# A hybrid decoder block on one core: the first norm by quarters behind the splitting of x, and one metered queue per stage for the work between weight units

## The chip, the core and the metric

The program runs on one core of a Trainium2 chip. A core has TensorE (PE, the matrix engine; its weight loads are shown apart as PEld), VectorE (DVE), ScalarE (ACT), GpSimd (POOL) and SyncE (SP, which here only issues DMAs). Each has its own instruction queue and works through it in order; they wait for each other by semaphores. The metric is the device time of one execution in microseconds (us). Before the change it is 1526.94 us, the median of three runs (1526.02 to 1527.0). What a measurement of this kernel can tell from no change is about 0.2%, or 3 us.

## What is computed

One decoder layer for 256 tokens with 2048 channels, all in float32: an RMSNorm, one large input projection, three parallel branches (an S5 state space, an RG-LRU recurrence and stick-breaking attention) that are gated and merged, an output projection with a residual, a second RMSNorm, an MLP with squared ReLU, and a last RMSNorm.

```python
def rms_norm(x, g):
    y = x * rsqrt(mean(x * x, axis=-1, keepdims=True) + EPS)
    return y * g

xn = rms_norm(x, norm_mix_g)
proj = xn @ w_in                          # 2048 -> 11264 columns
u_s5, u_lru, q, k, v, gate_logits = split(proj)
gates = sigmoid(gate_logits + b_gate)
# RG-LRU: causal conv of width 4, then
r, i = sigmoid(xc @ w_r + b_r), sigmoid(xc @ w_i + b_i)
a = exp(-8 * r * softplus(-lam))
y_lru = linear_scan(a, sqrt(1 - a * a) * (i * xc))
merged = g_s5 * (y_s5 @ w_br_s5) + g_lru * (y_lru @ w_br_lru) + g_attn * (y_attn @ w_br_attn)
h = x + merged @ w_out
hn = rms_norm(h, norm_mlp_g)
hdn = relu(hn @ w_up)                     # 2048 -> 8192
h = h + (hdn * hdn) @ w_down              # 8192 -> 2048
out = rms_norm(h, final_norm_g)
```

## The kernel before

**Units.** All large weights come as one stream of 520 units, each 256 rows by 512 columns of float32 (512 KB, tile `raw`, loaded on SP's queue by L130). Every unit is split in two parts whose sum carries the float32 precision: ACT casts `raw` to `hi` (L146) and DVE writes `lo = raw - hi` (L147). The activations are split in the same way (`xhi`/`xlo`, `hhi`/`hlo` and so on), and PE multiplies hi by hi, lo by hi and hi by lo. `raw`, `hi` and `lo` have three buffers each: `next_unit` (L151) loads up to three units ahead of the one in use and splits up to two ahead. So a unit's cast can start when PE is done with the unit three before it, its `lo` follows the cast, and its next load waits for the `lo` that frees the `raw` buffer.

**Chunks.** A chunk is 512 output columns. `chunk` (L195) puts channels on partitions, with 24 matmuls of 256 columns for a unit; `chunk_tok` (L215) and `pair_tok` (L245) put tokens on partitions, with 12 matmuls of 512 columns. `pair_tok` runs two chunks together, so that their last two units each come at the end. The order is: the two RG-LRU chunks of `w_in` (units 0 to 15), the two S5 chunks (16 to 31), the RG-LRU gate and branch chunks (gate 32 to 39, branch 40 to 43, and so on to 79), q, k and v, the attention gates and branches, the S5 gates and branches (to 231), `w_out` (232 to 263), and four quarters of the MLP, each four `w_up` chunks and four `w_down` chunks (the first `w_up` pair is units 264 to 279).

**Work between the chunks.** Everything else is written as Python generators that are put in the list `side` by `later(gens, rate)` (L164). After each unit's matmuls `pump` (L179) gives every task in that list `rate` steps (a step runs to the next `yield`), placed behind the unit's splits and matmuls. `finish(task)` runs a task to its end at once. So the amount of such work that goes between two `lo` instructions on DVE depends on how many tasks are in the list at that time, their rates, and how much a step holds. The tile scheduler then makes the final order for each engine from this program.

**The places that the change touches.** `norm1` (L349) waits eight units, then `square_sum` (L337) squares all of x in place on ACT and adds it up on DVE; a matmul with ones gives `ps_n1`, `rsqrt_mean` (L327) makes `rstd`, and `lru_in(0)` (L566) scales the first RG-LRU chunk out of PSUM (L373), which frees its two PSUM banks for the third chunk. `lru_half` (L510) is one half of RG-LRU: a convolution (L522, L524), two small matmuls for each 128 channels into `ps_l` (L530, L531), sigmoids (L532, L533), tanh (L537), exp (L542), sqrt (L550), scans (L557). `s5_scan` (L618) begins when the S5 chunks are done: sine tables (L593 to L598), the split of its first inputs into `ux` (L605, L606), and twelve small DMAs `stk<-ux` on SP's queue (L614); its first matmuls, `ps_v` (L638), read `stk`. `s5_load` and `s5_params` fetch S5's parameters and work them out, mostly on POOL.

Matmul results with tokens on partitions are turned into channels on partitions by `blocks` (L712): 16 DVE transposes of 32-row blocks for a chunk (L716), here in steps of four. `split_tok` does it for the merged branches, `residual` for the residual stream (then `residual_split`, L915), and `hidden` (L1005) for relu's output: transposes, the square on ACT (L1008, `hd_hi`), the same product on POOL (L1009), and the difference on DVE (L1012, `hd_lo`). Each chunk makes a `later` task of its own with rate 1.0, so two such tasks run side by side behind a pair.

Of the kernel before, what the change touches and what calls it, by code (L numbers as in the profile page):

```python
# [14 lines left out]
P = 128  # L15
# [31 lines left out]
def hybrid_block(ctx: ExitStack, tc: tile.TileContext, io, out):  # L47
# [142 lines left out]

    def finish(task):
        while step(task):
            pass
# [143 lines left out]
    def square_sum(t):  # L337
        for k in range(0, KT, 4):
            nc.scalar.activation(t[:, k:k + 4, :], t[:, k:k + 4, :], AF.Square)
            if k % 8:  # L340
                yield
        for k in range(0, 8, 4):
            nc.vector.tensor_tensor(t[:, k:k + 4, :], t[:, k:k + 4, :], t[:, k + 8:k + 12, :], ALU.add)
            yield
        for n in (4, 2, 1):
            nc.vector.tensor_tensor(t[:, 0:n, :], t[:, 0:n, :], t[:, n:2 * n, :], ALU.add)
        yield

    def norm1():  # L349
# [38 lines left out]
    def s5_load():  # L388
        nc.sync.dma_start(prm[:, 2, :], repeat(io["s5_log_dt"], 64))
        nc.sync.dma_start(prm[:, 0:2, :], io["s5_lam"])  # L390
        yield
        yield
        yield
        nc.sync.dma_start(cco, io["s5_c"])
        yield
        nc.sync.dma_start(bco, io["s5_b"])
        yield

    def s5_params():
# [3 lines left out]
        for _ in range(3):  # L403
            yield
# [158 lines left out]
    lq = later([lru_params()], 1)  # L563
# [317 lines left out]
    def split_tok(c, mT):  # L881
        yield
# [20 lines left out]
    last = later([split_tok(3, mlp.tile([P, 4, L], F32, tag="reluT", name="mT3", bufs=2))], 1.0)  # L903
# [5 lines left out]
    def ms(kt):  # L909
        if kt >= 12:  # L910
            finish(last)
# [7 lines left out]
    def residual(c):  # L919
        yield  # L920
        yield from blocks(h_tok[:, :, c * CH:(c + 1) * CH], hT[:, 4 * c:4 * c + 4, :], 4)
        for k in range(4 * c, 4 * c + 4):
            residual_split(k)
            if k % 2:
                yield

    rs2 = const.tile([P, 2], F32, name="rs2")
    rq = [None]

    def out_done(c, banks):  # L930
# [3 lines left out]
        rq[0] = later([residual(c)], 1.0)  # L934
# [5 lines left out]
    def hs(kt):  # L940
        if kt >= 12:
            finish(rq[0])
        return hhi[:, kt, :], hlo[:, kt, :]

    def norm2():
        while rq[0][0]:
            yield
        yield from square_sum(hT)
# [56 lines left out]
    def hidden(r, h_, l_, name):  # L1005
        rT = mlp.tile([P, 4, L], F32, tag="reluT", name=f"reluT{name}", bufs=2)
        yield from blocks(r, rT, 4)
        nc.scalar.activation(h_, rT, AF.Square)  # L1008
        nc.gpsimd.tensor_tensor(rT, rT, rT, ALU.mult)  # L1009
        yield  # L1010
        yield
        nc.vector.tensor_tensor(l_, rT, h_.bitcast(F32), ALU.subtract)  # L1012

    for q in range(NQ):
        hd, hq = {}, [None]

        def up_done(cu, banks):
# [9 lines left out]
            hq[0] = later([hidden(r, h_[:, k, :], l_[:, k, :], f"{q}_{c}")], 1.0)  # L1027
# [6 lines left out]
        def hs_(kt):  # L1034
            if kt >= 12:
                finish(hq[0])
# [90 lines left out]
```

## Time and profile before

| what | value |
|---|---|
| median of three runs | 1526.94 us |
| the profiled execution's own time | 1526.19 us |
| its span, first to last instruction | 1524.4 us |
| matmuls, PE | 7518 |
| bytes read from HBM | 282.71 MB, 187 GB/s over the span |
| DVE, ACT, POOL busy | 1172.1, 780.6, 66.3 us |

The profile shows one execution. A busy PE is not a PE at its peak: where the unit's operands are late, the matmuls simply start later, and the count of matmuls in a stretch tells more than the busy time. The program has two regular rhythms, 24 matmuls of 256 columns or 12 of 512 columns for a unit. In a table of stretches, each engine has its busy time with the number of its instructions behind it as (x...); then come the granted clock of TensorE as a share of full speed, the share of the DMA engines' time and the GB/s. In a timeline, a row is: start, duration, engine, line, operation, out<-in, number of merged instructions, and in brackets the idle time before it and what ended it.

### The profile page before, as it was taken

How to read it: one execution, taken by the hardware profiler on the slowest of the kernel's cores; microseconds unless marked ns; L12 is line 12 of the kernel's file. 1: busy time of each engine (PE TensorE's matmuls, PEld its weight loads, DVE VectorE, ACT ScalarE, POOL GpSimd, SP SyncE). 2: the span in 40 equal slices, each digit the busy share in tenths (PEclk: the TensorE clock that was granted, in tenths of full speed). 3: DMA queues.
4: the chain of work that ended last, by engine and by line, in shares of the span. 5: the costliest groups of instructions: out<-in, count | busy, mean ns of one | idle time of the engine just before them, and what ended most of it. 6: DMA issues, size and time to landing. Idle time of an engine off the chain costs nothing.

```text
span 1524.4 us, 19914 instructions
## 1 busy us (share of the span) xinstructions
PE 1492.2 (98%) x7518; PEld 1261.1 (83%) x7518; DVE 1172.1 (77%) x1452; ACT 780.6 (51%) x918; POOL 66.3 (4%) x76
## 2 busy tenths in 40 slices
PE   9898999999999999999999999999999999999997
PEld 9896888989887878987778778888888888888886
DVE  5786988887988989688698886468855787558855
ACT  7568556465765564444345444344433444344443
POOL 5000000000000000000000010000000000000011
PEclk9999999999999999999999999999999999999999
DMA  8554766655665657665756566656666666666564
GB/s 283 169 166 143 230 207 198 190 173 167 176 188 175 209 181 212 190 200 176 269 163 196 159 200 194 193 188 198 195 193 194 193 193 194 193 193 191 184 206 151
DMA packets 88914, 292.41 MB, mean 192 GB/s; under 512 B 12786, under 2 KB 17010, under 8 KB 88562
## 3 DMA queue, kind: packets, MB, share of 16 engines
q1 hardware_dynamic: 88386, 287.93, 61.5%
q10 hardware_dynamic: 432, 3.21, 0.6%
q8 instruction: 59, 0.97, 0.3%
q14 instruction: 37, 0.30, 0.1%
HBM read 282.71 MB, written 2.10 MB: 187 GB/s over the span
## 4 chain that ended last, share of the span: by engine, by line
PE 86%; DVE 7%; ACT 3%; DMA 2%; issue 2%; SPq 0%; DVEq 0%; ACTq 0%
PE mt_w_up L225 6%; PE mt_w_up L226 6%; PE mt_w_up L224 6%; PE mt_w_in L225 6%; PE mt_w_in L226 6%; PE mt_w_in L224 6%; PE mp_w_down L261 4%; PE mp_w_down L260 4%; PE mp_w_down L259 4%; PE mt_w_down L225 4%; PE mt_w_down L224 4%; PE mt_w_down L226 4%; PE mm_w_in L210 4%; PE mm_w_in L208 4%; PE mm_w_in L209 3%; DVE lo L147 3%
## 5 line engine op out<-in xcount | busy, mean ns | idle before, releaser
L147 DVE TENSOR_TENSOR lo<-raw,hi 128x1024 fp32r<-128x1024 f32 (+1 forms) x521 | 651.2, 1253 | 311.8 <-ACT hi L146 308.7
L146 ACT CAST hi<-raw 128x1024 fp32r<-128x1024 f32 (+1 forms) x521 | 545.7, 1049 | 642.5 <-PE mt_w_up L226 116.8
L225 PE MATMUL mt_w_up<-lo,hhi 128*128 128x512 f32 x448 | 174.9, 390 | 4.4 <-DVE lo L147 4.3
L225 PE MATMUL mt_w_in<-lo,xhi 128*128 128x512 f32 x448 | 176.2, 393 | 2.6 <-DVE lo L147 2.4
L224 PE MATMUL mt_w_in<-hi,xhi 128*128 128x512 f32 x448 | 175.9, 396 | 2.9 <-ACT hi L146 2.9
L226 PE MATMUL mt_w_in<-hi,xlo 128*128 128x512 f32 x448 | 175.4, 391 | 0.0
L226 PE MATMUL mt_w_up<-hi,hlo 128*128 128x512 f32 x448 | 174.3, 389 | 0.0
L224 PE MATMUL mt_w_up<-hi,hhi 128*128 128x512 f32 x448 | 174.3, 389 | 0.0
L208 PE MATMUL mm_w_in<-xhi,hi 128*128 128x256 f32 x512 | 146.5, 287 | 4.7 <-DVE rs L331 4.2
L210 PE MATMUL mm_w_in<-xhi,lo 128*128 128x256 f32 x512 | 145.4, 286 | 1.0 <-DVE lo L147 1.0
L209 PE MATMUL mm_w_in<-xlo,hi 128*128 128x256 f32 x512 | 145.5, 285 | 0.0
L716 DVE STREAM_TRANSPOSE reluT<-relu 32x256 f32<-32x256 f32 x256 | 111.5, 436 | 4.2
L208 PEld LDWEIGHTS mm_w_in<-xhi,hi 128*128 128x128 f32 x512 | 99.4, 194 | 5.5 <-issue 4.4
L225 PEld LDWEIGHTS mt_w_in<-lo,xhi 128*128 128x128 f32 x448 | 84.7, 189 | 23.1 <-DVE lo L147 6.5
L225 PEld LDWEIGHTS mt_w_up<-lo,hhi 128*128 128x128 f32 x448 | 84.1, 188 | 23.8 <-DVE lo L147 6.5
L225 PE MATMUL mt_w_down<-lo,hd_hi 128*128 128x512 f32 (+1 forms) x272 | 102.5, 377 | 0.0
L224 PE MATMUL mt_w_down<-hi,hd_hi 128*128 128x512 f32 (+1 forms) x272 | 102.4, 377 | 0.0
L226 PE MATMUL mt_w_down<-hi,hd_lo 128*128 128x512 f32 (+1 forms) x272 | 102.4, 376 | 0.0
L224 PEld LDWEIGHTS mt_w_in<-hi,xhi 128*128 128x128 f32 x448 | 84.4, 189 | 20.8 <-ACT hi L146 3.8
L210 PEld LDWEIGHTS mm_w_in<-xhi,lo 128*128 128x128 f32 x512 | 98.8, 194 | 1.5 <-DVE lo L147 1.4
L260 PE MATMUL mp_w_down<-lo,hd_hi 128*128 128x512 f32 x256 | 99.6, 389 | 0.0
L259 PE MATMUL mp_w_down<-hi,hd_hi 128*128 128x512 f32 x256 | 99.6, 389 | 0.0
(299 smaller groups left out, 2396.8 us busy)
## 6 DMA issues: line engine op xcount, KB each, us to landing
raw<-in_w_in SPq DMA_DIRECT2D x175, 512.0 KB, 4.2
raw<-in_w_up SPq DMA_DIRECT2D x128, 512.0 KB, 3.8
raw<-in_w_down SPq DMA_DIRECT2D x128, 512.0 KB, 3.9
raw<-in_w_out SPq DMA_DIRECT2D x32, 512.0 KB, 4.2
raw<-in_w_br_lru SPq DMA_DIRECT2D x16, 512.0 KB, 4.5
raw<-in_w_br_attn SPq DMA_DIRECT2D x16, 512.0 KB, 4.1
raw<-in_w_br_s SPq DMA_DIRECT2D x16, 512.0 KB, 4.1
stk<-ux SPq DMA_DIRECT2D x96, 64.0 KB, 4.1
```

The costliest lines, as they stand in the source:

```text
L146: anchor["act"] = nc.scalar.copy(h[:, k, :], r[:, k, :]).ins
L147: anchor["dve"] = nc.vector.tensor_tensor(l_[:, k, :], r[:, k, :], h[:, k, :].bitcast(F32), ALU.subtract).ins
L208: nc.tensor.matmul(o, wh[:, kk, s], xh, start=first and ct % 2 == 0, stop=False, skip_group_check=True)
L209: nc.tensor.matmul(o, wh[:, kk, s], xl, start=False, stop=False, skip_group_check=True)
L210: mm = nc.tensor.matmul(o, wl[:, kk, s], xh, start=False, stop=last and ct % 2 == 1, skip_group_check=True)
L224: nc.tensor.matmul(banks[j], xh[:, s], wh[:, a:b], start=kt == 0, stop=False)
L225: nc.tensor.matmul(banks[j], xh[:, s], wl[:, a:b], start=False, stop=False)
L226: return nc.tensor.matmul(banks[j], xl[:, s], wh[:, a:b], start=False, stop=kt == ng * UK - 1)
L259: nc.tensor.matmul(o, xh[:, s], wh[:, kk, :], start=kt == 0, stop=False)
L260: nc.tensor.matmul(o, xh[:, s], wl[:, kk, :], start=False, stop=False)
L261: mm = nc.tensor.matmul(o, xl[:, s], wh[:, kk, :], start=False, stop=kt == ng * UK - 1)
L716: nc.vector.transpose(d_[32 * a:32 * a + 32, :, :, 32 * b:32 * b + 32], s_[32 * b:32 * b + 32, :, :, 32 * a:32 * a + 32])
```

## The change

1. `norm1` no longer waits eight units. It squares x quarter by quarter on ACT, two units apart, and adds each quarter to the first on DVE, so that the small matmul comes three units earlier; `s5_load` starts seven units later and `s5_params` six. The RG-LRU task's rate goes from 1 to 1.15.
2. New helpers: `chained(task, gen)` appends a generator to one queue (and puts the queue in `side` if it isn't there), and sets a flag when that generator is through; `need(task, flag)` steps the queue only until that flag is set. `split_tok`, `residual` and `hidden` go in one queue each, with rates 1.5, 2.0 and 1.8, and their transposes come in steps of two.
3. The second norm's squares and adds go into `residual`, chunk by chunk; `norm2` has only the last two adds.
4. relu's product goes from POOL to DVE, and `ms`, `hs` and `hs_` ask with `need` for the chunk that a k-tile comes from.

```diff
+    def chained(task, gen):
+        flag = [False]
+        def run():
+            yield from gen(flag)
+            flag[0] = True
+        task[0].append(run())
+        if task not in side:
+            task[2] = 0.0
+            side.append(task)
+        return flag
+
+    def need(task, flag):
+        while not flag[0]:
+            assert step(task)
...
     def norm1():
-        for _ in range(8):
-            yield
-        yield from square_sum(xT)
+        yield
+        for k in range(0, KT, 4):
+            sq_ = xT[:, k:k + 4, :]
+            nc.scalar.activation(sq_, sq_, AF.Square)
+            yield
+            if k:
+                nc.vector.tensor_tensor(xT[:, 0:4, :], xT[:, 0:4, :], sq_, ALU.add)
+            yield
+        for n in (2, 1):
+            nc.vector.tensor_tensor(xT[:, 0:n, :], xT[:, 0:n, :], xT[:, n:2 * n, :], ALU.add)
+        yield
...
     def s5_load():
+        for _ in range(7):
+            yield
         nc.sync.dma_start(prm[:, 2, :], repeat(io["s5_log_dt"], 64))
...
         g.memset(ce, 0.0)
-        for _ in range(3):
+        for _ in range(9):
             yield
...
-    lq = later([lru_params()], 1)
+    lq = later([lru_params()], 1.15)
...
     def split_tok(c, mT):
-        yield
-        yield from blocks(m_tok[:, :, c * CH:(c + 1) * CH], mT, 4)
-        split_pair(4 * c, 4, mT)
+        def gen(flag):
+            yield
+            yield from blocks(m_tok[:, :, c * CH:(c + 1) * CH], mT, 2)
+            split_pair(4 * c, 4, mT)
+        return gen
...
+    mq, mf = [deque(), 1.5, 0.0], []
...
-            last = later([split_tok(c, pp.tile([P, 4, L], F32, tag="t3", name=f"mT{c}"))], 1.0)
-    finish(last)
+            mf.append(chained(mq, split_tok(c, pp.tile([P, 4, L], F32, tag="t3", name=f"mT{c}"))))
+    need(mq, mf[2])
...
     def residual(c):
...
+            flag[0] = True
+            sq_ = hT[:, 4 * c:4 * c + 4, :]
+            nc.scalar.activation(sq_, sq_, AF.Square)
+            yield
+            if c:
+                nc.vector.tensor_tensor(hT[:, 0:4, :], hT[:, 0:4, :], sq_, ALU.add)
                 yield
+        return gen
...
-    rq = [None]
+    rq, rfl = [deque(), 2.0, 0.0], {}
...
-        rq[0] = later([residual(c)], 1.0)
+        rfl[c] = chained(rq, residual(c))
...
     def hidden(r, h_, l_, name):
...
+            yield from blocks(r, rT, 2)
+            nc.scalar.activation(h_, rT, AF.Square)
+            nc.vector.tensor_tensor(rT, rT, rT, ALU.mult)
+            yield
+            yield
+            nc.vector.tensor_tensor(l_, rT, h_.bitcast(F32), ALU.subtract)
+        return gen
...
+    hq = [deque(), 1.8, 0.0]
...
-            hq[0] = later([hidden(r, h_[:, k, :], l_[:, k, :], f"{q}_{c}")], 1.0)
+            hf[c] = chained(hq, hidden(r, h_[:, k, :], l_[:, k, :], f"{q}_{c}"))
```

What the change makes of the engines' orders is seen at three places. The first is DVE in `w_out`, behind its pair of chunks; `lo250` is the `lo` of unit 250, L716 are the transposes of the residual, L917 the residual's own split. Before:

```order
L147 TENSOR_TENSOR lo250_6950<-raw250_6921,hi250_6949 128x1024
L716 STREAM_TRANSPOSE hT_6622<-h_tok_6625 32x2x4x32 x4
L147 TENSOR_TENSOR lo251_6972<-raw251_6947,hi251_6971 128x1024
L716 STREAM_TRANSPOSE hT_6622<-h_tok_6625 32x2x4x32 x8
L147 TENSOR_TENSOR lo252_6998<-raw252_6969,hi252_6997 128x1024
L716 STREAM_TRANSPOSE hT_6622<-h_tok_6625 32x2x4x32 x8
L147 TENSOR_TENSOR lo253_7024<-raw253_6995,hi253_7023 128x1024
L917 SCALAR_TENSOR_TENSOR hlo_6624<-hT_6622,par_79,hhi_6623 128x256 x2
L716 STREAM_TRANSPOSE hT_6622<-h_tok_6625 32x2x4x32 x4
L147 TENSOR_TENSOR lo254_7050<-raw254_7021,hi254_7049 128x1024
```

Now (L729 are the transposes, L932 the split):

```order
L147 TENSOR_TENSOR lo250_6952<-raw250_6923,hi250_6951 128x1024
L729 STREAM_TRANSPOSE hT_6622<-h_tok_6625 32x2x4x32 x4
L147 TENSOR_TENSOR lo251_6974<-raw251_6949,hi251_6973 128x1024
L729 STREAM_TRANSPOSE hT_6622<-h_tok_6625 32x2x4x32 x4
L147 TENSOR_TENSOR lo252_6996<-raw252_6971,hi252_6995 128x1024
L729 STREAM_TRANSPOSE hT_6622<-h_tok_6625 32x2x4x32 x2
L147 TENSOR_TENSOR lo253_7020<-raw253_6993,hi253_7019 128x1024
L932 SCALAR_TENSOR_TENSOR hlo_6624<-hT_6622,par_79,hhi_6623 128x256 x4
L147 TENSOR_TENSOR lo254_7043<-raw254_7017,hi254_7042 128x1024
L729 STREAM_TRANSPOSE hT_6622<-h_tok_6625 32x2x4x32 x2
L147 TENSOR_TENSOR lo255_7063<-raw255_7040,hi255_7062 128x1024
```

Before, two chunks' transposes stood together, eight between one `lo` and the next; now there are two or four, and the second chunk's come when the first's are through.

The second place is ACT in RG-LRU's second half; `hi37` is the cast of unit 37, `lru_r1`, `lru_i1`, `lru_tc1` and `lru_ts1` are this half's tiles, `ts0` and `tc0` the first S5 tables. Before, from the cast of unit 37 to that of unit 38, in the first gate chunk:

```order
L146 CAST hi37_1464<-raw37_1435 128x1024
L597 ACT_TABLE_LOAD
L597 ACTIVATE ts0_1403<-ts0_1403 128x1024
L598 ACTIVATE tc0_1402<-tc0_1402,half_pi_131 128x1024
L542 ACT_TABLE_LOAD
L542 ACTIVATE lru_r1_1224<-lru_r1_1224,nsp8_143 128x256 x2
L542 ACTIVATE lru_tc1_1227<-lru_tc1_1227,nsp8_143 128x256 x2
L605 CAST ux_102<-us5_99 128x256
L609 ACTIVATE ux_102<-bco_100,par_79 128x2x64 x2
L146 CAST hi38_1492<-raw38_1462 128x1024
```

Now, from behind the cast of unit 31 to that of unit 32 (L545 and L546 are the sigmoids, L550 tanh, L555 exp):

```order
L555 ACT_TABLE_LOAD
L555 ACTIVATE lru_r1_1070<-lru_r1_1070,nsp8_143 128x256
L545 ACT_TABLE_LOAD
L545 ACTIVATE lru_tc1_1073<-ps_l1_6_1285,par_79 128x256
L546 ACTIVATE lru_ts1_1074<-ps_l1_6_1285,par_79 128x256
L545 ACTIVATE lru_tc1_1073<-ps_l1_7_1290,par_79 128x256
L546 ACTIVATE lru_ts1_1074<-ps_l1_7_1290,par_79 128x256
L550 ACTIVATE lru_ts1_1074<-lru_tc1_1073,sp4_142 128x256 x2
L555 ACT_TABLE_LOAD
L555 ACTIVATE lru_r1_1070<-lru_r1_1070,nsp8_143 128x256
L555 ACTIVATE lru_tc1_1073<-lru_tc1_1073,nsp8_143 128x256 x2
L146 CAST hi32_1337<-raw32_1301 128x1024
```

The half has moved some five units forward, away from the S5 tables, and a table load that stood in one place for two parts now stands twice: exp of the first part, sigmoid of the second, exp again. In the whole program 31 table loads have become 33.

The third place is SP's queue where RG-LRU's branch begins; `raw40` is the load of unit 40, the branch's first, and `stk<-ux` are S5's small DMAs. Before:

```order
L130 DMA raw38_1462<-in_w_in 128x1024
L130 DMA raw39_1490<-in_w_in 128x1024
L130 DMA raw40_1526<-in_w_br_lru 128x1024
L614 DMA stk_103<-ux_102 32x2x256
L614 DMA stk_103<-ux_102 32x512
```

Now, from the first of the small DMAs to the load of unit 40:

```order
L627 DMA stk_103<-ux_102 32x2x256
L130 DMA raw39_1508<-in_w_in 128x1024
L627 DMA stk_103<-ux_102 32x512
L627 DMA stk_103<-ux_102 32x2x256 x2
L627 DMA stk_103<-ux_102 32x512
L627 DMA stk_103<-ux_102 32x2x256 x2
L627 DMA stk_103<-ux_102 32x512
L627 DMA stk_103<-ux_102 32x2x256 x2
L627 DMA stk_103<-ux_102 32x512
L627 DMA stk_103<-ux_102 32x2x256
L130 DMA raw40_1538<-in_w_br_lru 128x1024
```

Before, the loads of units 39 and 40 stood ahead of the small DMAs, and that of unit 41 behind the last of them; now unit 39's load stands behind the first of them and unit 40's behind the last.

More of the change, by code (lines that the diff above doesn't have):

```diff
@@ L902, in hybrid_block @@
     nc.scalar.dma_start(x_tok, io["x_res"])
-    last = later([split_tok(3, mlp.tile([P, 4, L], F32, tag="reluT", name="mT3", bufs=2))], 1.0)
+    mf.append(chained(mq, split_tok(3, mlp.tile([P, 4, L], F32, tag="reluT", name="mT3", bufs=2))))
     hT = act.tile([P, KT, L], F32, tag="m16", name="hT")
@@ L909, in ms @@
     def ms(kt):
-        if kt >= 12:
-            finish(last)
+        need(mq, mf[kt // 4])
         h_, l_ = mg[kt // 8]
@@ L940, in hs @@
     def hs(kt):
-        if kt >= 12:
-            finish(rq[0])
+        need(rq, rfl[kt // 4])
         return hhi[:, kt, :], hlo[:, kt, :]
     def norm2():
-        while rq[0][0]:
+        while rq[0]:
             yield
-        yield from square_sum(hT)
+        for n in (2, 1):
+            nc.vector.tensor_tensor(hT[:, 0:n, :], hT[:, 0:n, :], hT[:, n:2 * n, :], ALU.add)
+        yield
         a = hT[:, 0, :]
@@ L1034, in hs_ @@
         def hs_(kt):
[L1035 to L1036 removed]
+            need(hq, hf[kt // 4])
             h_, l_ = hd[kt // 8]
```

35 lines of the change are left out of this document (11 added, 24 removed).

## Prediction

> **What bounds the kernel now.** The page's first lines come first: span and busy shares.
>
> ```profile
> span 1524.4 us, 19914 instructions
> PE 1492.2 (98%) x7518; PEld 1261.1 (83%) x7518; DVE 1172.1 (77%) x1452; ACT 780.6 (51%) x918; POOL 66.3 (4%) x76
> ```
>
> PE is the bound, and the change leaves its matmuls as they are. It can gain only where PE is late, and 98% hides that, since matmuls that start late overlap less. So I read the table of stretches of 25 us next and count matmuls (columns: stretch, length, then PE, PEld, DVE, ACT and POOL busy with counts, granted clock, DMA share, GB/s).
>
> ```profile
> 50.00:75.00 25.00, 20.78 (x149) 20.34 (x148) 19.29 (x34) 12.08 (x17) 0.00 (x0) 0.86 0.46 141
> 75.00:100.00 25.00, 25.00 (x204) 24.79 (x204) 19.10 (x25) 20.05 (x30) 0.00 (x0) 1.00 0.49 155
> ...
> 125.00:150.00 25.00, 20.14 (x82) 15.52 (x81) 15.65 (x22) 21.78 (x31) 0.00 (x0) 0.93 0.44 132
> 150.00:175.00 25.00, 25.00 (x110) 19.96 (x109) 23.78 (x27) 11.22 (x14) 0.00 (x0) 1.00 0.77 228
> ...
> 675.00:700.00 25.00, 24.87 (x109) 19.95 (x108) 23.80 (x40) 10.54 (x10) 0.00 (x0) 1.00 0.53 172
> 700.00:725.00 25.00, 23.48 (x103) 18.77 (x102) 20.06 (x26) 11.07 (x12) 0.00 (x0) 1.00 0.61 190
> ...
> 775.00:800.00 25.00, 22.50 (x91) 17.85 (x90) 23.43 (x39) 11.41 (x16) 0.00 (x0) 0.93 0.55 162
> ...
> 850.00:875.00 25.00, 21.62 (x93) 16.96 (x92) 22.32 (x41) 10.96 (x14) 1.89 (x1) 1.00 0.44 137
> 875.00:900.00 25.00, 23.98 (x104) 19.18 (x103) 22.82 (x30) 12.30 (x13) 3.38 (x2) 1.00 0.63 189
> ...
> 1200.00:1225.00 25.00, 25.00 (x112) 20.71 (x111) 21.73 (x31) 11.90 (x13) 1.89 (x1) 1.00 0.63 192
> ```
>
> A full stretch holds 112 long matmuls (last row), so one costs 0.223 us and a unit of 12 takes 2.68; of the 256-column kind it holds 204 (second row), 0.1225 each, 2.94 for a unit of 24. What is missing is the loss. First norm: 204 - 149 = 55, 6.7 us. RG-LRU's second half: 112 - 82 = 30 and 2 behind it, 7.1, and as eight of the 82 are S5's short ones, 0.1 less each, 8.0. Last branches: 3 + 9, 2.7. `w_out`: 21, 4.7. First `w_up` pair: 19 + 8, 6.0. That is 28 us in all that the change could reach. The waits say who is late (engine, line, awaited; us, times, longest).
>
> ```profile
> PE mt_w_up L225 <- DVE lo L147: 4.3, 2, 3.4
> PE mm_w_in L208 <- DVE rs L331: 4.2, 1, 4.2
> ...
> PE mt_w_out L225 <- DVE lo L147: 2.5, 2, 1.8
> ```
>
> DVE delivers `lo` late because other work stands ahead of it, or it delivers rstd late. The rest of each loss is slower matmuls, seen in the clock of 0.86 beside the norm.
>
> **First norm: -5.2.** PE waits 4.2 us for `rs`, since PSUM's two banks for the third chunk come free only in `lru_in(0)`. The matmul with ones now stands three units, 8.8 us, earlier, more than the 4.2 us: the wait goes, and with it the half-clock matmuls behind it, together the 6.7. What is late next is DVE. RG-LRU's first half comes on top of the loads of S5's parameters.
>
> ```profile
> 85.79 0.68 DVE L545 SCALAR_TENSOR_TENSOR lru_th<-lru_r,lru_th 128x512 f32<-128x512 f32 x1
> ...
> 94.07 1.27 DVE L557 TENSOR_TENSOR_SCAN lru_xc<-lru_r,lru_i 128x256 f32<-128x256 f32 x2
> 95.25 1.20 DVE L147 TENSOR_TENSOR lo<-raw,hi 128x1024 fp32r<-128x1024 f32 x1
> ...
> 99.87 1.52 DVE L524 SCALAR_TENSOR_TENSOR lru_xc<-ulru,par,lru_xc 128x255 f32<-128x255 f32 x3
> ```
>
> From `lo19` to `lo26` the new order has 20 instructions of 0.68 us or near it and 6 of the convolution at 0.5, 16.6 us, and the eight `lo` of 1.2, 9.6: 26.2 us, where PE needs 8 x 2.94 = 23.5. Between no loss, if the lead at the start carries it, and all 2.7, I take 1.5, the middle. The norm's adds are the same elements in another order, and ACT's squares have the cover of a unit in which it is busy 1.04 for the cast.
>
> **RG-LRU's second half: +1.2.** Before, ACT did a burst between two casts, and SP's queue was full.
>
> ```profile
> 124.64 1.04 ACT L146 CAST hi<-raw 128x1024 fp32r<-128x1024 f32 x1
> 125.70 1.28 ACT L597 ACT_TABLE_LOAD   x1
> ...
> 132.90 2.92 ACT L146 CAST hi<-raw 128x1024 fp32r<-128x1024 f32 x3
> ```
>
> ```profile
> 126.97 0.33 SPq L130 DMA_DIRECT2D raw<-in_w_br_lru  x1
> 133.01 7.80 SPq L614 DMA_DIRECT2D stk<-ux  x12
> 140.92 1.50 SPq L130 DMA_DIRECT2D raw<-in_w_br_lru  x3
> ```
>
> The casts stopped for 132.90 - 125.68 = 7.2 us, and the twelve small DMAs held SP for 7.8, so that unit 41 was loaded at 140.92. The burst now stands between `hi31` and `hi32`: three table loads of 1.28 and ten activations.
>
> ```profile
> 115.22 1.28 ACT L532 ACT_TABLE_LOAD   x1
> 116.52 0.47 ACT L532 ACTIVATE lru_r<-ps_l,par 128x256 f32<-128x256 f32 x1
> 116.89 0.47 ACT L533 ACTIVATE lru_i<-ps_l,par 128x256 f32<-128x256 f32 x1
> ```
>
> One follows the other after 0.37, so the burst lasts 3 x 1.28 + 10 x 0.37 = 7.6. Three buffers cover three units less the cast and the `lo`, 3 x 2.9 - 1.0 - 1.2 = 6.5; 1.1 us is left; a second split ahead may cover some, and I leave 0.7. Scans and S5's tables on DVE (1.2 each by the row of `lo`, of equal size) delay units 35 and 36 by some 2.0.
>
> > The Trainium skill ("ScalarE: Activation LUTs", What ACT_TABLE_LOAD costs) puts a switch at 1283 ns for the load and 1380 ns for a drain. The row speaks against the drain, as the sigmoid begins 1.30 us after its load. By the rule, three loads would make the burst 4.1 us longer, and the sum 1513.4 by that.
>
> Then the queue: unit 40's load now stands behind the last small DMA. These wait for `ux`, which by the new order on ACT and DVE is ready about a cast and a `lo`'s half before unit 38 begins, 1.2 us. Unit 40 is ready 7.8 + 0.33 for the issues, 4.2 for the load and 1.05 for the cast after `ux`, 13.4, so 12.2 us after unit 38 begins.
>
> ```profile
> raw<-in_w_in SPq DMA_DIRECT2D x175, 512.0 KB, 4.2
> ```
>
> PE wants it after two units, 5.4 us, and the late splits of units 38 and 39 (0.5) are in that: a wait of some 6.5. So 0.7 + 2.0 + 6.5 = 9.2 stand against 8.0: +1.2. Bounds: -8.0, if casts and loads were early enough for all of it, and +4, if `ux` is a unit later than I read.
>
> > The Trainium skill ("TensorE: Matmul & The Clock Gate", Part 1) has the clock fall to half after an idle window of about 3.4 us in a free-running grid. The first stretch above agrees, 0.86 beside a wait of 4.2; that of 850:875 stays at 1.00 beside one of 3.4. By the rule the wait at unit 40 would be followed by a window at half clock, 1.7 more, and the sum 1511.0 by that.
>
> **Last branches: -2.7.** Before, twelve transposes stood in one run:
>
> ```profile
> 695.32 5.37 DVE L716 STREAM_TRANSPOSE mT<-merged 32x256 f32<-32x256 f32 x12
> ```
>
> Now two or four, 0.9 to 1.8 us between one `lo` and the next. With the `lo`'s 1.2 that is below a unit's 2.68, so the whole loss goes; below that bound lies none of it.
>
> **`w_out`: -4.2.**
>
> ```profile
> 769.83 1.23 DVE L147 TENSOR_TENSOR lo<-raw,hi 128x1024 fp32r<-128x1024 f32 x1
> 771.09 3.58 DVE L716 STREAM_TRANSPOSE hT<-h_tok 32x256 f32<-32x256 f32 x8
> 774.69 1.22 DVE L147 TENSOR_TENSOR lo<-raw,hi 128x1024 fp32r<-128x1024 f32 x1
> ...
> 780.73 0.88 DVE L917 SCALAR_TENSOR_TENSOR hlo<-hT,par,hhi 128x256 fp32r<-128x256 f32 x2
> ...
> 792.29 1.28 DVE L933 TENSOR_TENSOR h_tok<-mt_w_out,xres 128x512 f32<-128x512 f32 x2
> ```
>
> Eight transposes and a `lo` take 4.8 us, more than 2.68; this goes, and the 4.7 with it. But the second norm's adds come in here: from `lo248` to `lo275` stand 28 `lo` at 1.2, 64 transposes at 0.45, 16 splits at 0.44, 8 residuals at 0.64 and the adds, 4.4 (three chunks' and the last two, at a `lo`'s rate): 33.6 + 28.8 + 7.0 + 5.1 + 4.4 = 78.9. PE takes 28 x 2.68 = 75.0 and DVE starts with a lead of a unit or more. I leave 0.5 of wait; bounds none and the 3.9 of the difference.
>
> **First `w_up` pair: -6.0.**
>
> ```profile
> 865.00 3.61 DVE L716 STREAM_TRANSPOSE reluT<-relu 32x256 f32<-32x256 f32 x8
> 868.63 2.71 DVE L147 TENSOR_TENSOR lo<-raw,hi 128x1024 fp32r<-128x1024 f32 x1
> 868.37 1.89 POOL L1009 TENSOR_TENSOR reluT<-reluT 128x1024 f32<-128x1024 f32 x1 [829.21 <-DMA raw<-in_w_up]
> ...
> 1028.66 1.23 DVE L147 TENSOR_TENSOR lo<-raw,hi 128x1024 fp32r<-128x1024 f32 x1
> ```
>
> Two `hidden` tasks side by side put eight transposes, 3.6 us, in front of a `lo`. In one queue, a chunk's 16 transposes (7.2), eight `lo` (9.8), product and difference (1.2 each) make 19.4 us of DVE in 8 x 2.68 = 21.4 of PE: it fits, and the 6.0 goes; the bound is half of it, should the queue's bunches of four still push a `lo`. The product on DVE is new there: 1.2 us, sixteen times, 19. But beside POOL's product the `lo` took 2.71 instead of 1.23, so 1.5 of each 1.2 comes back, and DVE is no longer loaded by it than before. In the three later quarters the cover is DVE's idle time, 3.3 of 25 us in the last stretch above; without it, each of the 16 would cost up to 1.2. I take nothing.
>
> **The sum.** -5.2 + 1.2 - 2.7 - 4.2 - 6.0 = -16.9. The profiled execution lasted 1526.2 us, 1.8 of it around the span, which the change leaves alone; 0.7 below the median of 1526.9. 1526.2 - 16.9 = **1509.3**. About 0.2%, 3 us, is what can be told from no change.
>
> **The rivals.**
>
> *RG-LRU's wait is worse than before.* The unit-40 wait, table loads in the burst, half-clock matmuls behind it: +4 for `ux` a unit late and 2 for the slower matmuls, in the measure of the first norm, where 6.7 lost stood beside a wait of 4.2: 1515.3. For it speaks that SP's queue is in order and the twelve issues last 7.8 us; against, that ACT no longer holds S5's first tables and exp in one burst. A table switch that held ACT for twice its load would do it too, 3 x 1.28 = 3.8 more in the burst: 1513.1; the sigmoid 1.30 us behind its load speaks against that. Chance 0.17 for both. The second is what the rule on switches in the Trainium skill's "ScalarE: Activation LUTs" would make of it.
>
> *VectorE becomes the bound.* If `w_out`'s 3.9 is paid in full and half of the 6.0 stays, 3.4 + 3.0 more: 1515.7. For it: 78.9 us of work against 75.0. Against: DVE is at 23.4 of 25 there already and runs ahead when nothing is bunched. Chance 0.12.
>
> *RG-LRU's loss goes altogether.* If `ux` is ready two units earlier than I read, the small DMAs end before unit 40's load is due; -8.0 stands for +1.2: 1500.1. For it: the half moved five units forward. Against: the first small DMA still stands ahead of unit 39's load. Chance 0.10.
>
> *The change doesn't do what it says.* The losses behind the chunks are not DVE's bunches but late loads:
>
> ```profile
> 785.65 1.05 ACT L146 CAST hi<-raw 128x1024 fp32r<-128x1024 f32 x1 [4.91 <-DMA raw<-in_w_out]
> ```
>
> ACT waits for a load in the midst of `w_out`'s loss. Then those 2.7 + 4.7 + 6.0 stay and only the norm's part moves: 1526.2 - 5.2 + 1.2 = 1522.2. Against it: a load waits for the `lo` that frees its buffer, and that stood behind the transposes. Chance 0.04.
>
> *Slower.* `need` and the rates put S5's small DMAs ahead of a load in each of S5's eight blocks, not in the first alone. With each load a unit later than its lead of two units (5.4 us, against 7.8 of issues) PE loses 2.7 each time, 8 x 2.7 = 21.6 less the 16.9: 1530.9. It decides as soon as the issues stand ahead of a load that is due within 5.4 us. Against: from unit 53 on SP's rows are the same as before. Chance 0.04.
>
> **How the numbers follow.** The forecast has 0.53. Faster by over 0.2%, below 1523.1: forecast, the two that cost some of it, the one that gains, and the unchanged losses (1522.2, so half of it): 0.94. Within 0.2%: 0.02; slower: 0.04. I move 0.03 to the middle for mixtures of the costs: 0.91, 0.05, 0.04. The range reaches from the gain in RG-LRU (1500) to both costs at once in part, 1520; each term's bounds, -8 to +4 at RG-LRU, 3.9 in `w_out` and 3 in `w_up`, lie in it unless they come together.
>
> **What the profile after would show.** The first norm: no wait for `rs`, at least 195 matmuls in 50 to 75, and `lo` the awaited thing up to unit 26. RG-LRU: the longest wait of PE for ACT's `hi` of unit 40, behind a load that SP issues right behind twelve small DMAs; without it the -8.0 case holds. Last branches, `w_out` and `w_up`: no stretch under 108 matmuls but the one with the load of x, and no row of eight transposes. relu: POOL's 1.9 us rows gone, no `lo` over 2 us beside them, and 110 to 112 matmuls in the later quarters; 105 would show that DVE is full. Wrong it would be, above all, if the counts there stay while the order of DVE changed: then loads, not `lo`, set the time.

## The result, and the profile after

The changed kernel takes 1517.69 us, median of four runs (1516.25 to 1519.39), against 1526.53 us of the kernel before in the same rounds: a ratio of 0.9943, 95% interval 0.9931 to 0.9956. It is 8.8 us faster. The forecast was 1509.3 us, so about half of the expected 16.9 us came. Its profiled execution took 1518.29 us. The first lines of its page:

```profile
span 1516.4 us, 19895 instructions
PE 1489.1 (98%) x7518; PEld 1260.0 (83%) x7518; DVE 1176.4 (78%) x1468; ACT 783.9 (52%) x920; POOL 35.1 (2%) x60
```

The table of stretches of the changed kernel, with the columns as before:

```profile
50.00:75.00 25.00, 24.56 (x192) 23.94 (x191) 19.77 (x29) 19.51 (x34) 7.87 (x15) 1.00 0.50 162
75.00:100.00 25.00, 22.91 (x173) 22.43 (x173) 23.07 (x36) 13.50 (x17) 0.00 (x0) 0.93 0.55 170
...
125.00:150.00 25.00, 21.19 (x82) 16.38 (x81) 14.56 (x18) 16.84 (x22) 0.00 (x0) 0.86 0.60 193
675.00:700.00 25.00, 25.00 (x112) 20.71 (x111) 23.41 (x37) 10.33 (x10) 0.00 (x0) 1.00 0.55 173
700.00:725.00 25.00, 24.97 (x110) 20.33 (x110) 22.41 (x32) 11.52 (x12) 0.00 (x0) 1.00 0.69 228
775.00:800.00 25.00, 24.85 (x110) 20.25 (x109) 24.34 (x39) 13.46 (x16) 0.00 (x0) 1.00 0.61 188
800.00:825.00 25.00, 24.06 (x105) 19.19 (x104) 24.37 (x41) 11.66 (x14) 0.00 (x0) 1.00 0.59 178
825.00:850.00 25.00, 22.65 (x103) 18.48 (x102) 16.01 (x22) 13.87 (x18) 0.00 (x0) 1.00 0.60 188
850.00:875.00 25.00, 25.00 (x112) 20.71 (x111) 23.06 (x35) 11.65 (x13) 0.00 (x0) 1.00 0.59 187
875.00:900.00 25.00, 25.00 (x112) 20.71 (x111) 24.01 (x36) 12.02 (x14) 0.00 (x0) 1.00 0.62 188
1200.00:1225.00 25.00, 25.00 (x112) 20.71 (x111) 21.56 (x29) 12.58 (x14) 0.00 (x0) 1.00 0.64 201
```

The holes at 700, 775, 850 and 875 are closed. The one at 125 stays (82 in both). New ones stand at 75 (173 of 204, where the kernel before had all 204), 800 (105, before 112) and 825 (103, before 113). The waits of PE in the changed kernel (engine, line, awaited; us, times, longest):

```profile
PE mm_w_in L227 <- DVE lo L147: 4.7, 5, 1.9
PE mt_w_in L242 <- DVE lo L147: 3.4, 5, 1.8
PE ps_n L977 <- DVE hT L972: 2.3, 1, 2.3
...
PE mt_w_br_lru L241 <- ACT hi L146: 2.0, 1, 2.0
```

The wait for `rs` is gone. In its place PE waits for `lo`, five times in the first chunks, and once 2.3 us for `hT`, at the small matmul of the second norm.

Since the stretches slide against each other, I compare two kernels by when PE begins each weight unit: the first matmul of unit n, read from PE's timeline, minus that of the kernel before (us; negative is ahead). The columns behind the second are experiments, told below.

| unit | before starts at | changed | norm 1 undone | norm 2 later | conv. spread | both | both, norm 1 later |
|---|---|---|---|---|---|---|---|
| 13 | 45.7 | +0.2 | +0.1 | +0.9 | +0.1 | +0.9 | +0.2 |
| 24 | 88.2 | -4.6 | +0.6 | -4.0 | -5.6 | -4.7 | -5.8 |
| 32 | 111.2 | +3.0* | +0.6 | +3.3* | -4.3 | -3.6 | -3.9 |
| 44 | 156.2 | +0.9 | +0.6 | +1.4 | -4.2 | -3.5 | -6.1 |
| 222 | 688.5 | -0.2 | -0.6 | +0.2 | -4.5 | -4.4 | -6.0 |
| 248 | 764.1 | -2.4 | -2.6 | -2.1 | -7.0 | -6.2 | -8.1 |
| 276 | 845.0 | -2.0 | -0.6 | -4.4 | -3.5 | -8.4 | -10.3 |
| 300 | 916.8 | -8.2 | -6.7 | -10.5 | -9.6 | -14.5 | -16.4 |
| 519 | 1510.2 | -8.0 | -6.5 | -10.3 | -9.4 | -14.3 | -16.2 |

*Here the second half's 16 small matmuls (3.4 us of PE's work) stand ahead of unit 32, in the other columns behind it.

In the changed kernel's column two gains are lost again: 4.6 us by unit 24, gone by unit 44; and 4.7 between units 252 and 254, gone by unit 276. The 2.5 between 222 and 248 and the 6.1 between 276 and 300 stay. The two places where most is lost are seen in DVE's timeline of the changed kernel (start, duration, engine, line, operation). At units 25 and 26:

```profile
85.77 1.20 DVE L147 TENSOR_TENSOR lo<-raw,hi 128x1024 fp32r<-128x1024 f32 x1
86.89 0.69 DVE L573 TENSOR_TENSOR ylru_lo<-lru_tc,ylru_hi 128x512 fp32r<-128x512 f32 x1
87.49 2.45 DVE L537 SCALAR_TENSOR_TENSOR lru_xc<-ulru,par,lru_xc 128x255 f32<-128x255 f32 x6
89.86 1.28 DVE L386 TENSOR_TENSOR us<-mm_w_in,rstd 128x512 f32<-128x512 f32 x2
91.05 1.22 DVE L147 TENSOR_TENSOR lo<-raw,hi 128x1024 fp32r<-128x1024 f32 x1
```

From one `lo` to the next lie 5.3 us, where a unit takes 2.9: two steps of the convolution at once, and the scaling of an S5 chunk. At units 273 and 274, PE first, then DVE:

```profile
831.93 0.39 PE L277 MATMUL mp_w_up<-lo,hhi 128*128 128x512 f32 x1
834.66 0.58 PE L977 MATMUL ps_n<-ones,hT 128*128 128x1 f32 x4 [2.35 <-DVE hT L972]
835.10 0.48 PE L278 MATMUL mp_w_up<-hi,hlo 128*128 128x512 f32 x1
```

```profile
831.10 1.23 DVE L947 TENSOR_TENSOR hT<-hT 128x1024 f32<-128x1024 f32 x1
832.36 0.69 DVE L972 TENSOR_TENSOR hT<-hT 128x512 f32<-128x512 f32 x1
832.97 1.22 DVE L147 TENSOR_TENSOR lo<-raw,hi 128x1024 fp32r<-128x1024 f32 x1
834.10 0.42 DVE L972 TENSOR_TENSOR hT<-hT 128x256 f32<-128x256 f32 x1
```

PE's queue is in order, and the small matmul stands in it before the last add has run, with a `lo` between the two adds. All matmuls of `w_up` behind it wait, though nothing needs the norm's result before `w_down`. Unit 274 starts 3.1 us late by that: 2.35 of wait, and 0.7 for the small matmuls themselves, which the kernel before pays at unit 277.

### The profile page after: what moved, and what is told of

It reads as the page before. It is cut to its first block, busy times and chain, and to the rows that moved or that the text cites. A ratio compares the mean times of both kernels' runs of the same rounds, so it can differ in the third digit from the quotient of the medians.

```text
span 1516.4 us, 19895 instructions
## 1 busy us (share of the span) xinstructions
PE 1489.1 (98%) x7518; PEld 1260.0 (83%) x7518; DVE 1176.4 (78%) x1468; ACT 783.9 (52%) x920; POOL 35.1 (2%) x60
## 4 chain that ended last, share of the span: by engine, by line
PE 81%; DVE 11%; issue 4%; ACT 2%; DMA 2%; SPq 0%; DVEq 0%; ACTq 0%
PE mt_w_up L242 6%; PE mt_w_up L243 6%; PE mt_w_up L241 6%; PE mt_w_in L242 5%; PE mt_w_in L243 5%; PE mt_w_in L241 5%; DVE lo L147 4%; PE mt_w_down L242 4%; PE mt_w_down L241 4%; PE mt_w_down L243 4%; PE mp_w_down L277 4%; PE mp_w_down L278 4%; PE mp_w_down L276 4%; PE mm_w_in L227 4%; PE mm_w_in L225 4%
## 5 line engine op out<-in xcount | busy, mean ns | idle before, releaser
L147 DVE TENSOR_TENSOR lo<-raw,hi 128x1024 fp32r<-128x1024 f32 (+1 forms) x521 | 638.2, 1226 | 289.4 <-ACT hi L146 285.6
L729 DVE STREAM_TRANSPOSE reluT<-relu 32x256 f32<-32x256 f32 x256 | 111.5, 435 | 4.2
L278 PE MATMUL mp_w_down<-hi,hd_lo 128*128 128x512 f32 x256 | 99.6, 389 | 0.0
L226 PEld LDWEIGHTS mm_w_in<-xlo,hi 128*128 128x128 f32 x512 | 99.2, 194 | 0.1
```

Source lines behind the costliest of these rows:

```text
L147: anchor["dve"] = nc.vector.tensor_tensor(l_[:, k, :], r[:, k, :], h[:, k, :].bitcast(F32), ALU.subtract).ins
L226: nc.tensor.matmul(o, wh[:, kk, s], xl, start=False, stop=False, skip_group_check=True)
L278: mm = nc.tensor.matmul(o, xl[:, s], wh[:, kk, :], start=False, stop=kt == ng * UK - 1)
L729: nc.vector.transpose(d_[32 * a:32 * a + 32, :, :, 32 * b:32 * b + 32], s_[32 * b:32 * b + 32, :, :, 32 * a:32 * a + 32])
```

## The experiments

Every time stands beside the kernel before on the same chip; a kernel's runs spread over 1 to 5 us, so the places are read from the traces.

**Is the first part worth anything?** The changed kernel with `norm1` as before, `s5_load` and `s5_params` starting when they did, and the rate back:

```diff
-    lq = later([lru_params()], 1.15)
+    lq = later([lru_params()], 1)
...
     def norm1():
-        yield
-        for k in range(0, KT, 4):
...
+        for _ in range(8):
+            yield
+        yield from square_sum(xT)
```

> The changed kernel with its first part undone: the first norm, the delays of the S5 loads and parameters and the RG-LRU task's rate are those of before; the queues, the second norm and relu's product stay as changed. Theory A (read from the two traces): the first part was worth about nothing, since the wait for rs was replaced by waits for lo at units 13, 14 and 26 with half-clock matmuls behind them; up to unit 44 the changed kernel stands 0.9 us behind. Then this kernel takes 1517 us, within 1.5 us of the changed kernel's 1517.7. Theory B (as predicted): the first part gains 4.0 us and the shortfall lies elsewhere. Then this kernel takes 1521 to 1522 us.

It takes 1519.21 us, ratio 0.9952 (0.9936 to 0.9969), which no interval separates from the changed kernel's 0.9943. At unit 44 it stands +0.6, the changed kernel +0.9. The loss of the kernel before is back at its old place in the undone kernel, and the one at 75 is away:

```profile
50.00:75.00 25.00, 20.39 (x145) 19.90 (x144) 20.49 (x36) 12.88 (x18) 0.00 (x0) 0.86 0.45 145
75.00:100.00 25.00, 25.00 (x204) 24.79 (x203) 18.54 (x24) 19.83 (x29) 0.00 (x0) 1.00 0.48 161
```

So theory A holds for the place: as the change has it, the first part gains nothing by unit 44; it only moves the loss. The median is 1.5 us above the changed kernel's first one, at the edge of what theory A allowed; in the traces the difference arises at unit 274, 700 us later, where the clock fell in this run and not in that of the changed kernel (last section).

**The second norm's matmul.**

```diff
     def norm2():
...
-        yield
+        for _ in range(3):
+            yield
         a = hT[:, 0, :]
```

> The changed kernel with the small matmul of the second norm two units later, behind unit 275 instead of unit 273. Theory A: PE, whose queue is in order, stood 2.5 us at that matmul while the last two adds and a lo were still to come on DVE, and lost 3.1 us at unit 273; two units later the adds are through and the 3.1 us go: 1514.6 us. Theory B: VectorE is some units behind there anyway, and lo of units 274 to 276 is late as soon as PE no longer stands at the small matmul: 1516.5 to 1517.7 us, with a wait for lo in place of the one for hT.

It takes 1515.96 us, 0.9938 (0.9923 to 0.9953). In its trace the stretch is full, and the only wait of PE between 800 and 860 is one of 0.9 us at unit 266 that the changed kernel has too:

```profile
825.00:850.00 25.00, 25.00 (x114) 20.73 (x113) 17.55 (x24) 15.10 (x19) 0.00 (x0) 1.00 0.62 204
```

From unit 264 to 276 it gains 2.6 us on the changed kernel: 3.1 at unit 274, less 0.5 in the two units behind, where the small matmuls now stand. Theory A holds but for those; a median of 1.7 less is within what the runs spread.

**The bunch at unit 26.**

```diff
                     nc.vector.scalar_tensor_tensor(xc[:, j, s:], ...)
+                    if c and s < 3:
+                        yield
                 yield
+        if c:
+            lq[1] = 1.5
         yield
```

> The changed kernel with the convolution of RG-LRU's second half in steps of one tap instead of three, and that task's rate 1.5 behind it, so that four instructions of VectorE fewer stand between lo of units 25 and 26. Theory A: the loss of 5.6 us at units 25 to 27 comes from that one bunch (5.3 us of VectorE for a unit of 2.9): PE waits 2.1 us, and the matmuls behind the wait run at half clock. Then units 25 to 27 lose at most 1 us, with no half-clock window there. Theory B: VectorE is full on average from unit 19 on (26 us of work for 23.5), and spreading moves the wait to another unit: at least 3 us are still lost between units 24 and 30. The second half then runs some units later, beside S5's tables, and may give back up to 4 us there, so the stretch of units 24 to 30 decides, not the total: 1513 to 1518 us.

At units 24 to 26 PE now loses 1.3 us instead of 4.1 (the 5.6 of the expectation held 1.5 us of the second half's small matmuls, which stand in unit 27 of the changed kernel), and the clock stays at 1.00: the same stretch has 200 matmuls instead of 173.

```profile
75.00:100.00 25.00, 24.16 (x200) 23.75 (x199) 22.42 (x32) 13.48 (x17) 0.00 (x0) 1.00 0.59 191
```

That is a little over the 1 us that theory A allowed, and far under the 3 of theory B. By unit 44 it stands 5.1 us ahead of the changed kernel, so the later second half gives nothing back. DVE was busy 22.4 us of the 25, against 23.1: nearly the same load in smaller pieces, so it was the bunch, not the average. How much the bunch costs depends on the clock. The kernel with the product on GpSimd (the next run) has the same bunch, order and wait of 1.9 us as the changed kernel, but the clock stays at 1.00 behind it, and it loses 2.3 us at these units; so some 1.0 of the 2.8 gained is the shorter wait, and most of the other 1.8 a stretch at half clock that didn't come. The total, 1516.88 us, 0.9941 (0.9926 to 0.9956), hardly shows it, since this kernel loses more at unit 274:

```profile
825.00:850.00 25.00, 22.68 (x89) 18.37 (x88) 12.80 (x16) 11.27 (x14) 0.00 (x0) 0.86 0.51 167
```

The order and the wait are those of the changed kernel, 103 matmuls at 1.00; here the clock fell behind the wait.

**Relu's product.**

```diff
-            nc.vector.tensor_tensor(rT, rT, rT, ALU.mult)
+            nc.gpsimd.tensor_tensor(rT, rT, rT, ALU.mult)
```

> The changed kernel with relu's product back on GpSimd, all else as changed. Theory A (as predicted): the product on VectorE costs what it gives back at the lo beside it (1.2 us against about 1.5), and VectorE's idle time hides the rest: within 1 us of 1517.7. Theory B: VectorE has no room in the first quarter, so that this kernel is 1.5 us or more faster there. Theory C: the product on GpSimd makes lo late even with one queue, so that this kernel is 2 us or more slower, at the units beside a product.

1520.62 us, 0.9971 (0.9961 to 0.9981): slower than the changed kernel by some 3 us, as theory C has it. From unit 288 on its trace falls back by 3.8 us against the kernel before, the changed kernel by 0.6. The place is where the first quarter's `w_up` ends and its `w_down` begins. There are a stretch, a group (line, engine, operation; busy us, mean ns; idle before, awaited), PE's waits from 870 on, and rows of DVE's timeline:

```profile
900.00:925.00 25.00, 22.66 (x98) 17.96 (x97) 20.75 (x27) 11.73 (x12) 3.79 (x2) 1.00 0.50 167
```

```profile
L1039 DVE TENSOR_TENSOR hd_lo<-reluT,hd_hi 128x1024 fp32r<-128x1024 f32 x16 | 19.4, 1215 | 3.8 <-POOL reluT L1036 3.8
```

```profile
PE mp_w_down L277 <- DVE lo L147: 2.3, 2, 1.7
```

```profile
885.29 1.23 DVE L1039 TENSOR_TENSOR hd_lo<-reluT,hd_hi 128x1024 fp32r<-128x1024 f32 x1 [1.84 <-POOL reluT L1036]
886.43 1.22 DVE L147 TENSOR_TENSOR lo<-raw,hi 128x1024 fp32r<-128x1024 f32 x1
...
901.90 2.15 DVE L147 TENSOR_TENSOR lo<-raw,hi 128x1024 fp32r<-128x1024 f32 x1 [2.06 <-ACT hi L146]
903.97 1.21 DVE L1039 TENSOR_TENSOR hd_lo<-reluT,hd_hi 128x1024 fp32r<-128x1024 f32 x1
```

Two things are seen. `hd_lo` waits for POOL in DVE's queue with a `lo` behind it, 1.84 us at 885 and 1.91 at 922; there the kernel falls back by 0.6 and 1.0 us. And at 902 the `lo` beside a product takes 2.15 us instead of 1.23; PE waits 1.7 us for it, and 2.1 us are lost in that one unit, against 0.4 in the changed kernel. That `lo` also began late, behind a cast (2.06 us of idle time), so the 2.1 isn't all the product's. The -5.6 us between units 284 and 288 is there in this kernel as well, so the queue, without the product's move, closes the hole of the first `w_up` pair.

**Both mended at once, and two steps more.** Four kernels on one chip in the same rounds: the second norm later and the convolution spread; that, and the first norm's DVE part one unit behind ACT's; or that, and S5's first twelve small DMAs on GpSimd's queue; and the changed kernel once more.

```diff
     def norm1():
...
-        rsqrt_mean(rstd, ps[:, 0:L], L)
-        rsqrt_mean(rstd_tok, ps[:, L:L + 2], 2)
+        halves = [rsqrt_mean2(rstd, ps[:, 0:L], L), rsqrt_mean2(rstd_tok, ps[:, L:L + 2], 2)]
+        yield
+        for h_ in halves:
+            h_()
         lru_in(0)
```

Here `rsqrt_mean2` issues ACT's instruction and returns a function that issues the three of DVE. For the queue, with `b=0` for the first block:

```diff
-            nc.sync.dma_start(stk[i * 32:i * 32 + 32, t].bitcast(F32), ...)
+            (nc.sync if b else nc.gpsimd).dma_start(stk[i * 32:i * 32 + 32, t].bitcast(F32), ...)
```

> The changed kernel with the second norm's small matmul two units later and the second half's convolution spread, both at once. Theory A: the two losses are independent, 700 us apart; with 2.3 us gone at unit 274 and 5.1 us up to unit 44 (each as the single run showed it in its trace), this takes 1510.3 us, about what was predicted of the change. Theory B: the gain up to unit 44 is chance of the clock's half-speed stretches, and the total stays near 1514 to 1516 us.

> As the run with both, and the first norm's VectorE part one unit behind its reciprocal square root, so that lo of unit 13 isn't queued behind instructions that wait for ACT. Theory A: the 2.4 us lost at units 13 and 14 are that queueing, and go: 1508 us. Theory B: the scaling of the first chunk (lru_in) is then a unit later and the third chunk waits for its banks, or VectorE's load behind it makes the same loss at units 14 to 16: 1510 us or more.

> As the run with both, and the first block's twelve small DMAs (stk from ux) issued on GpSimd's queue instead of SP's, so that no load of a unit stands behind them. Theory A (as predicted for that place): the 7.9 us of issues hold back the loads of units 40 and 41, and the 3 us lost at units 39 to 41 go: 1507.5 us. Theory B: PE waits there for S5's small matmuls in its own queue, which read what those DMAs bring, or for casts behind ACT's burst; then the units 37 to 41 lose the same, 1510 us, or more if GpSimd issues more slowly than SP's 0.65 us each.

> The changed kernel once more, on the same chip and in the same rounds as the three runs beside it. Both theories: 1517.7 us within 1 us; its trace shows the lost time at the same places (units 13 to 16, 25 to 28, 35 to 41 and 273), while the places of the half-clock stretches may differ.

| kernel | us | ratio | 95% interval |
|---|---|---|---|
| changed, again | 1519.33 | 0.9948 | 0.9932 to 0.9964 |
| both | 1513.75 | 0.9909 | 0.9895 to 0.9924 |
| both, norm 1 later | 1511.51 | 0.9896 | 0.9881 to 0.991 |
| both, GpSimd's queue | 1511.76 | 0.99 | 0.9883 to 0.9916 |

Both together are 5.6 us below the changed kernel in the same rounds, more than the single totals add up to (1.7 and 0.8 below its first median); in the trace, 1510.2 us of span against 1516.4 and, again, 1518.7. In the trace both places are mended, as theory A has it; of the 1510.3 us that it expected, the median of 1513.75 lacks 3.5 and lies nearer to theory B's 1514 to 1516, so the total decides for neither. The changed kernel itself came out 1.6 us above its first median, outside the 1 us that was expected: its trace has the same waits at the same places, and one stretch at half clock more, behind unit 273 (0.82 over that unit).

With the first norm's DVE part later, units 13 and 14 lose 0.3 us, instead of 1.7 in the run with both and 2.6 in the changed kernel. What had blocked there is in the changed kernel's timeline of DVE:

```profile
39.06 1.24 DVE L147 TENSOR_TENSOR lo<-raw,hi 128x1024 fp32r<-128x1024 f32 x1 [0.21 <-ACT hi L146]
42.92 0.43 DVE L347 SCALAR_TENSOR_TENSOR rs<-rs 128x256 f32<-128x256 f32 x1 [2.62 <-ACT rs L346]
...
46.60 1.49 DVE L147 TENSOR_TENSOR lo<-raw,hi 128x1024 fp32r<-128x1024 f32 x1
```

DVE waited 2.62 us for ACT's `rs` and had seven instructions of the norm and of `lru_in` ahead of the next `lo`. But 0.9 us of that came back at units 15 and 16, where the third chunk's banks are now later, and 1.0 at unit 26, where the pieces of the second half fall otherwise, as theory B had it: by unit 32 the run is 0.4 us ahead of the one with both. It is 2.7 ahead by unit 44, away from the edit's own place; what in the shifted second half gives that wasn't tried apart. The medians differ by 2.2 us, with overlapping intervals.

With the small DMAs off SP's queue, units 39 to 41 take 11.0 us instead of 13.3 in the run with both. The loads no longer stand behind them, and PE's waits in the branch chunk (units 40 and 41) shrink from the first two rows to the third:

```profile
PE mt_w_br_lru L242 <- DVE lo L147: 1.5, 2, 0.9
PE mt_w_br_lru L241 <- ACT hi L146: 0.9, 1, 0.9
```

```profile
PE mt_w_br_lru L242 <- DVE lo L147: 0.7, 1, 0.7
```

So at its place 2.3 of theory A's 3 us go. The waits for casts in the gate chunk ahead of it stay at 1.6 us; but behind the same waits of 1.0 and 0.5 us at unit 38 the clock fell here (0.70 over that unit, 1.00 in the run with both), which cost 1.4 us, and between units 32 and 44 only 0.5 us is left. Eleven of the twelve issues last 5.9 us on POOL; all twelve last 7.9 on SP.

All four edits at once:

> The run with both, the first norm's VectorE part a unit later and the first block's small DMAs on GpSimd's queue, all four at once. Theory A: what the last two gave adds up (2 us at units 13 to 15, about 0.5 us between units 32 and 44): 1511 us, a little below the 1511.5 of the best run so far. Theory B: both edits take away from the same late splits at units 37 to 41, and this equals the best run within 1 us.

1510.99 us, 0.9904 (0.9888 to 0.9921), the same as the best of the others within the spread; the total fits both theories. In the trace nothing is lost at units 13 and 14, but PE waits 2.5 us for a cast at unit 42, with the clock at 0.56 over that unit, and between units 32 and 44 the run falls 2.5 us behind the one with norm 1 later. So the two gains don't add up in it. What stands after the experiments is some 1511 us, 15 us below the kernel before.

## Why the prediction went as it did

The sign was right, the range held the time, and the likeliest value was 8 us too low. Term by term, from the starts of units:

| term | forecast | measured |
|---|---|---|
| first norm (to unit 32, without the small matmuls) | -5.2 | -0.5 |
| RG-LRU's second half (to unit 44) | +1.2 | +1.4 |
| last branches (222 to 232) | -2.7 | -2.5 |
| `w_out` with the second norm (248 to 276) | -4.2 | +0.4 |
| first `w_up` pair (276 to 300) | -6.0 | -6.1 |
| not in the sum: 44 to 222, x's load (232 to 248), behind 300 | 0 | -1.2 + 0.4 + 0.2 |

The forecasts add up to -16.9, the measured to -7.9. Some of the measured sizes are the clock's: in the kernel with the product on GpSimd, with the same order on PE, DVE and ACT up to 150 us, the first row is -2.7, mostly because the clock didn't fall behind unit 26.

**First norm.** The 6.7 that should go by the earlier matmul was 4.6: the wait for `rs` went, as said, but DVE now waited for the same `rs` with a `lo` behind it. I had asked what the norm's chain delays on PE, not what it holds up in DVE's own queue. And the 1.5 for DVE's load behind it was mis-sized: 4.1 were lost, above the upper bound of 2.7 (2.3 where the clock stayed up). I had added eight units' work and compared the sums; the loss comes from the largest piece between two `lo`, 5.3 us for a unit of 2.9. The run with the convolution spread shows it: nearly the same sum, 1.3 us lost instead of 4.1.

**`w_out`.** The loss in the pair went, -4.7, as the rows of transposes said. The 0.5 for DVE's load in it was 2.0 (0.4 up to unit 264, 1.6 behind it), within its bounds of none to 3.9. What no term held was the 3.1 at unit 274: I counted the second norm's adds as DVE's work and forgot the matmul that reads them in PE's queue; the kernel before lost 0.7 there, at unit 277, so 0.7 of the next row's gain is only that matmul's move. To name, for every wait, what is queued behind the waiting instruction on its engine would have found both.

**RG-LRU's second half** came out nearly right by chance. I had 6.5 us of wait at unit 40 behind the small DMAs; it was 2.0, and 1.8 for `lo` at unit 36, with matmuls at half clock behind both (0.86 in that stretch). SP's queue and ACT around unit 40:

```profile
131.71 7.04 SPq L627 DMA_DIRECT2D stk<-ux  x11
138.79 1.56 SPq L130 DMA_DIRECT2D raw<-in_w_br_lru  x3
```

```profile
141.59 1.31 ACT L745 ACTIVATE gate<-gate 128x512 f32<-128x512 f32 x2 [5.18 <-DVE gate L744]
142.81 2.13 ACT L146 CAST hi<-raw 128x1024 fp32r<-128x1024 f32 x2
```

The chain was as I named it: the load right behind the last small DMA, landed at 142.5, the cast done at 143.8, 12.1 us after `ux` against my 13.4. What failed is the lead: `ux` was ready 4.1 us before unit 38 began, not 1.2, as PE itself was late by then. One thing I didn't name: the gates' sigmoid, which needs the end of unit 39, stands ahead of that cast in ACT's queue and ended 0.4 us after the load had landed. In this order an earlier load alone would not have shortened the wait, so it has two causes, and my sum knew one. In the run with both, moving the DMAs off SP's queue took 2.3 us from units 39 to 41; the casts of units 40 and 41 then stood ahead of the sigmoid.

**Last branches** were right, size and reason. **The first `w_up` pair** came to its size, and the queue closes its hole, as the run with the product on GpSimd shows. **The product** I took at nothing; undone, it costs some 3 us, and that row is -3.7 instead of -6.1. So the row's size needs the product's move as well, and this term was mis-sized.

Two signs I had set for the stretches were missed as well: 192 matmuls between 50 and 75 instead of 195 or more, and 105 and 103 where no stretch but that of x was to be under 108.

Of the rivals, "VectorE becomes the bound" came nearest, with 1515.7 us, but not at its places: the holes in `w_up` closed. That VectorE is late with a bunch in front of it, and PE late behind a matmul that waits for VectorE, are closer to the truth than a full engine.

## What to carry to other kernels

Between two deliveries that the bound engine waits for, look at the largest piece of other work, not at the average load. When a result is made earlier, go through every in-order queue its consumers stand in, and give a waiting instruction of little urgency a place at which its operands are surely there. A gain in one place that vanishes in the total should be followed unit by unit through the trace before it is believed to be absent.

## What the runs showed of the hardware

The same wait costs differently from run to run, by what the clock does behind it. Around unit 26 the changed kernel and the one with the product on GpSimd have the same order. Stretches of 3.4 us of the changed kernel, then of the other:

```profile
89.00:92.40 3.40, 1.48 (x13) 1.28 (x11) 3.40 (x7) 1.45 (x2) 0.00 (x0) 1.00 0.25 95
92.40:95.80 3.40, 3.40 (x17) 3.40 (x18) 3.40 (x7) 0.00 (x0) 0.00 (x0) 0.52 0.54 173
```

```profile
89.00:92.40 3.40, 1.49 (x13) 1.29 (x12) 3.40 (x5) 1.04 (x1) 0.00 (x0) 1.00 0.07 14
92.40:95.80 3.40, 3.40 (x30) 3.40 (x29) 3.38 (x8) 1.05 (x1) 0.00 (x0) 1.00 0.80 273
```

Both have 13 matmuls in the stretch of the wait. Behind it one runs 17 at a clock of 0.52, the other 30 at 1.00: 13 matmuls of 0.12 us, 1.6 us. The run of the changed kernel again fell like the first (20 matmuls at 0.57). At the second norm's matmul the same 2.3 us of wait cost 3.1 us with the clock at 1.00, and 103 matmuls in its stretch, but it left 89 at 0.86 in the kernel with the convolution spread, quoted above, and in the one with the first norm undone:

```profile
825.00:850.00 25.00, 22.67 (x95) 18.32 (x94) 15.81 (x22) 12.03 (x15) 0.00 (x0) 0.93 0.53 177
```

The Trainium skill ("TensorE: Matmul & The Clock Gate", Part 1) says that the window is free-running and the half clock follows an idle window of some 3.4 us. A free-running window agrees with these traces: in the changed kernel the clock is at half from 92.55 to 95.97, from 130.10 to 133.51 and from 143.75 to 147.17 us, each 3.41 us long and whole multiples of 3.41 apart. On that grid the changed kernel's wait at unit 26 lies within one step (89.14 to 92.55), while in the other kernel an edge at 90.97 (counted back from its own half-clock stretch at 142.17) cuts it. That PE be idle for a whole window doesn't agree, as 13 matmuls ran in the step ahead of the drop, with PE busy 1.49 of its 3.41 us; the other kernel's step up to 90.97 has 1.68 and no drop. Where the limit lies these runs don't tell. In the traces the waits and this together account for why the single edits don't add up; the timed runs have no trace, and there it stays open.
